# A hybrid diffusion step on one core: a planner with measured durations, load latencies and changes of matmul kind, and small products that are held back

## The chip, the cores and the metric

The kernel runs on one core of a Trainium2 chip. The metric is the device time of one execution in microseconds (us). Three executions of the kernel before took 1000.77, 1001.39 and 1002.3 us; the median is 1001.39 us.

## The reference, cut to what matters

A two-layer backbone is applied once to 128 context tokens and 256 latent tokens with shared weights (model width 1024). All 384 tokens are three tiles of 128 rows, t = 0 (context), 1 and 2 (latent).

```python
def trunk_layer(x, mod, p, lb_f, lb_b, rope, ctx_k, ctx_v, s0_f, s0_b):
    sh1, sc1, g1, sh2, sc2, g2 = jnp.split(mod, 6, axis=-1)      # mod = silu(c) @ w_mod + b_mod
    h = rmsnorm(x, p['norm1_g']) * (1 + sc1) + sh1
    proj = h @ p['w_in']                                          # 1024 -> 3328 columns
    q_r, f_f, f_b, i_r, g_r, q_a, k_a, v_a = jnp.split(proj, ...)
    ...
    o_f, s_f = gla_chunked(qr, -jnp.expm1(lf_f), vr, lf_f, s0_f)  # 4 recurrent heads, both directions
    o_b, s_b = gla_chunked(qr[:, ::-1], ...)
    ...
    o_a = attend_blocks(qa, k_all, v_all)                         # 8 query heads on 2 key heads
    x = x + g1 * (jnp.concatenate([o_r, o_a], axis=-1) @ p['w_out'])
    h2 = rmsnorm(x, p['norm2_g']) * (1 + sc2) + sh2
    x = x + g2 * (jnp.square(jax.nn.relu(h2 @ p['w1'])) @ p['w2'])   # 1024 -> 4096 -> 1024
```

The modulation `mod` needs 6144 columns of `w_mod` per layer for only two rows (`c_ctx` and `c`). The outputs are both normalised token sets, the keys and values of the context tokens, and their final recurrent states.

## The kernel before, in words

**Dense products.** A weight tile of 128 x 1024 numbers (512 KB) is loaded by SyncE into one of four `raw` buffers. ScalarE writes its high part as `hi` (L358), VectorE the rest as `lo` (L366), both in the type fp32r. Each product is then three fp32r matmuls: high by high, low by high, high by low. These are the lines L570 and L571 (queries and keys of the attention heads), L589 (the recurrent heads' features), L548 (their values and gates), L620 (w_out), L1124 and L1139 (w1) and L1150 (w2). They are called dense below.

**Small products.** The rest of TensorE's work is short groups in fp32: the modulation rows L413 (four products of `cT` with a raw `w_mod` tile, 256 columns each), L402 (the same rows where VectorE has summed them first at L382), the levels of the recurrence L936 and L922, its states and outputs L1011, L1034 to L1038, the attention scores L769 (fp32r on half of the array) and L807 and values L837, and transposes: L424, L494, L672, L731, L732, L791, L826, L1005, L1058, L1179. The trace shows two records for most of the fp32 products that the program holds, so eight at L413 are one weight tile's four.

**What sets the order.** Nothing on the chip decides: the program of each engine is a fixed list. It is written by a planner, `Sched`, when the kernel is built. Every piece of work is a step `S(engine, duration, function, r, w, acq, rel)`: keys that it reads and writes, buffers that it takes and gives back. Steps stand in chains (generators), and every chain has a priority. `start_of` (L51) works out when a chain's next step could start, from the free time of its engine, from the times of its keys plus a latency by engine (`LAT`), and from the free times of its buffers. `run` (L71) takes the earliest candidate, on VectorE, ScalarE and GpSimd with a window in which the priority counts (`BIAS`), calls its function, which emits the instructions, and books the time. A load is booked as busy for its duration on SyncE, and its data are taken to be there 1.6 us later: 1.47 us and 1.6 us for a 512 KB tile (L351).

**Around the change.** `load_chain` (L345) issues the weight tiles in one fixed order, each as soon as a `raw` buffer is free. A tile of `w_mod` gives its buffer back when L413 has read it; a tile of another weight when its `lo` is written. In layer 0 the tiles of three modulation blocks (eight each) stand between the tiles of `w_in`; the other blocks are summed by VectorE during the MLP of layer 0 (`mod_acc`, L382) and come to TensorE as L402. At the start a chain of matmuls on zeros (`warm_chain`, L272) keeps TensorE busy until the first dense product can run.

Of the kernel before, what the change touches and what calls it, by code (L numbers as in the profile page):

```python
# [14 lines left out]
NT = 3  # L15
# [5 lines left out]
LAG = HEAD + 1  # L21
WOT = 6
# [3 lines left out]
class Sched:  # L26


    LAT = {"PE": 0.2, "DVE": 0.19, "ACT": 0.13, "POOL": 0.15, "SP": 0.1}

    def __init__(self):
        self.free = {}
        self.t = {}
        self.slots = {}
        self.bound = {}
        self.chains = []
        self.n = 0

# [12 lines left out]
    def start_of(self, st):  # L51
        eng, dur, fn, r, w, acq, rel, key = st
        s = self.free.get(eng, 0.0)
        for k in r:
# [3 lines left out]
            s = max(s, te + (self.LAT[e] if e != eng else 0.0))  # L58
# [8 lines left out]
        return s  # L67

    BIAS = {"PE": (0.03, 0.0), "DVE": (0.96, 0.255), "ACT": (0.6, 0.255), "POOL": (0.8, 0.3), "SP": (0.03, 0.0)}

    def run(self):  # L71
        while self.chains:
            cand = []
            for c in self.chains:
                s = self.start_of(c[3])
                if s is not None:
                    cand.append((s, c))
            if not cand:
                raise RuntimeError("stuck: " + repr([(c[0], c[3][0], c[3][7], [k for k in c[3][3] if k not in self.t], c[3][5]) for c in self.chains]))
            pr = lambda c: c[0]() if callable(c[0]) else c[0]  # L80
            m, c = min(cand, key=lambda a: (a[0], pr(a[1]), a[1][1]))
            lim, w = self.BIAS[c[3][0]]
            s, c = min(((s, d) for s, d in cand if d[3][0] == c[3][0] and s <= m + lim), key=lambda a: ((a[0] - m if w else 0.0) + w * pr(a[1]), pr(a[1]), a[0], a[1][1]))
            eng, dur, fn, r, w, acq, rel, key = c[3]
# [6 lines left out]
            e = s + dur  # L91
            self.free[eng] = e
            lat = 0.0
            if eng == "SP":
                lat = 1.6
            for k in w:
                self.t[k] = (e + lat, eng)
            for name in rel:
                cls, o, i = self.bound.pop(name)
                self.slots[cls].append((e + lat, i, o))  # L100
# [7 lines left out]
def S(eng, dur, fn, r=(), w=(), acq=(), rel=(), key=None):  # L108
    return (eng, dur, fn, tuple(r), tuple(w), tuple(acq), tuple(rel), key)
# [10 lines left out]
def c_r(n):  # L120
    return max(n / 2400.0, 0.107)


def c_f(n, m=128):
    return max(n / 600.0, 0.214 * m / 128) + 0.004


def step_kernel(tc, A):
# [86 lines left out]
    def start_chain():  # L215
        yield S("SP", 0.9, lambda: SP.dma_start(out=cst, in_=A["cst"]), w=["smalls", "ident"])
# [20 lines left out]
        for t in range(NT):  # L237
            yield S("SP", 1.5, ldx(t), w=[("x", 0, t, 0), ("x", 0, t, 1)])

    def const_chain():  # L240
# [4 lines left out]
        yield S("SP", 2.0, ld2, r=[("rawk", 0, "feat", W_R0["q"])], acq=[("t2", "mraw")], w=["consts0"])  # L245
# [1163 lines left out]
```

## Time and profile before

| what | value |
|---|---|
| times of three executions, us | 1000.77, 1001.39, 1002.3 |
| profiled execution, us | 1002.09 |
| its span, from first to last instruction, us | 1000.3 |
| TensorE matmul busy, us (share) | 980.1 (98%) |
| VectorE busy, us (share) | 680.7 (68%) |
| ScalarE busy, us (share) | 495.6 (50%) |
| mean granted TensorE clock | 0.997 |
| moved by DMA | 165.40 MB, 165 GB/s over the span |

The span counts from the first to the last instruction; the profiled execution's own time is 1.8 us longer. PE is TensorE's matmul, PEld its weight loads, which overlap; DVE is VectorE, ACT ScalarE, POOL GpSimd, SP SyncE. A matmul's row gives its start, its length and what it reads and writes; since matmuls are pipelined, the distance between two starts tells what one costs, not its length. Where an engine sat idle before an instruction, the row ends with that time and with what released it.

### The profile page before, as it was taken

Reading aid. Unit: us, or ns where it says so; the run is one execution under the profiler, and the core shown is the slowest. Engines: PE = TensorE matmul, PEld = TensorE weight load, DVE = VectorE, ACT = ScalarE, POOL = GpSimd, SP = SyncE. Lnnn points to the kernel's source line nnn. Section 1 sums busy time; section 2 is a strip of 40 time slices with the busy share of each in tenths; the row PEclk is TensorE's granted clock in tenths of the full one; section 3 lists DMA queues with packets and bytes.
Section 4 is the critical chain, followed back from the end, with each engine's and each line's share of the span. In section 5 each row is a group of like instructions: output and inputs, shape, how many; then the busy total and the mean of one; then the engine's idle time right before and its main releaser. Section 6 shows DMA issues by size and latency. Waiting matters only on the chain.

```text
span 1000.3 us, 17353 instructions
## 1 busy us (share of the span) xinstructions
PE 980.1 (98%) x6925; PEld 836.4 (84%) x6925; DVE 680.7 (68%) x1169; ACT 495.6 (50%) x903; POOL 51.9 (5%) x49
## 2 busy tenths in 40 slices
PE   8999999999999999999999999999999999999997
PEld 5785677888989889888888978888899999999895
DVE  3687676687888889887746887977765444434434
ACT  4456644455544444444345677646564444444432
POOL 0020000111000000000011200011100000000002
PEclk9999999999999999999999999999999999999999
DMA  9958556333578767776615332242446544454611
GB/s 311 319 164 254 172 186 192 96 116 113 173 251 265 238 218 243 233 228 214 221 48 166 105 100 64 86 120 93 127 127 191 167 128 148 147 147 148 190 43 64
DMA packets 140657, 165.40 MB, mean 165 GB/s; under 512 B 5872, under 2 KB 105616, under 8 KB 140064
## 3 DMA queue, kind: packets, MB, share of 16 engines
q1 hardware_dynamic: 140576, 164.29, 53.0%
q8 instruction: 54, 0.88, 0.4%
q14 instruction: 27, 0.22, 0.1%
HBM read 161.35 MB, written 2.92 MB: 164 GB/s over the span
## 4 chain that ended last, share of the span: by engine, by line
PE 76%; DMA 11%; DVE 7%; issue 2%; ACT 2%; SPq 0%; POOL 0%; POOLq 0%; DVEq 0%; ACTq 0%
PE bank L1124 19%; PE bank L1150 19%; PE bank L589 9%; DMA raw<-w_mod_d 8%; PE bank L548 6%; PE bank L620 6%; DVE t L382 4%; PE bank L570 3%; PE bank L413 2%; PE bank L936 1%; PE bank L571 1%; DVE lo L366 1%; PE bank L1139 1%; PE bank L837 1%; DMA raw<-w_in_d 1%
## 5 line engine op out<-in xcount | busy, mean ns | idle before, releaser
L358 ACT CAST hi<-raw 128x1024 fp32r<-128x1024 f32 (+1 forms) x152 | 155.5, 1028 | 141.2 <-DMA raw<-w_d 69.4
L366 DVE TENSOR_TENSOR lo<-raw,hi 128x1024 fp32r<-128x1024 f32 (+1 forms) x152 | 179.6, 1192 | 44.9 <-ACT hi L358 44.5
L382 DVE SCALAR_TENSOR_TENSOR t<-raw,cT,t 128x512 f32<-128x512 f32 x196 | 135.4, 746 | 32.8 <-DMA raw<-w_mod_d 32.6
L1124 PE MATMUL bank<-mA,hi 128*128 128x384 f32 (+1 forms) x336 | 112.0, 333 | 0.0
L1124 PE MATMUL bank<-mA,lo 128*128 128x384 f32 (+1 forms) x336 | 111.1, 331 | 0.0
L1124 PE MATMUL bank<-mB,hi 128*128 128x384 f32 (+1 forms) x336 | 110.9, 330 | 0.0
L1112 DVE TENSOR_TENSOR mB<-t,mA 128x384 fp32r<-128x384 f32 x64 | 35.6, 556 | 96.0 <-ACT mA L1111 95.9
L1150 PE MATMUL bank<-lo,mA 128*128 128x512 f32 x252 | 98.8, 392 | 0.0
L1150 PE MATMUL bank<-hi,mB 128*128 128x512 f32 x252 | 98.7, 392 | 0.0
L1150 PE MATMUL bank<-hi,mA 128*128 128x512 f32 x252 | 98.0, 389 | 0.0
L1109 ACT ACTIVATE t<-bank 128x384 f32<-128x384 f32 x64 | 31.4, 490 | 125.3 <-PE bank L1124 122.8
L1124 PE MATMUL bank<-mA,wts 128*128 128x384 f32 (+1 forms) x352 | 88.7, 326 | 0.0
L1150 PE MATMUL bank<-wts,mA 128*128 128x512 f32 x264 | 87.7, 392 | 0.0
L358 ACT CAST wts<-raw 128x1024 fp32r<-128x1024 f32 x44 | 46.1, 1050 | 56.8 <-DMA raw<-w_d 21.3
L589 PE MATMUL bank<-Hh,hi 128*128 128x384 f32 x192 | 69.7, 363 | 0.6 <-ACT hg L866 0.6
L366 DVE TENSOR_TENSOR wts<-raw,wts 128x1024 fp32r<-128x1024 f32 x44 | 54.1, 1237 | 22.0 <-ACT wts L358 21.9
L1124 PEld LDWEIGHTS bank<-mA,hi 128*128 128x128 f32 x336 | 63.2, 188 | 3.1 <-issue 1.3
L589 PE MATMUL bank<-Hh,lo 128*128 128x384 f32 x192 | 64.8, 337 | 0.0
L589 PE MATMUL bank<-Hl,hi 128*128 128x384 f32 x192 | 64.6, 337 | 0.0
L1124 PEld LDWEIGHTS bank<-mB,hi 128*128 128x128 f32 x336 | 63.2, 188 | 1.4
L1124 PEld LDWEIGHTS bank<-mA,wts 128*128 128x128 f32 x352 | 62.5, 188 | 1.2 <-issue 0.4
L1124 PEld LDWEIGHTS bank<-mA,lo 128*128 128x128 f32 x336 | 63.2, 188 | 0.0
(252 smaller groups left out, 1955.5 us busy)
## 6 DMA issues: line engine op xcount, KB each, us to landing
raw<-w_d SPq DMA_DIRECT2D x128, 512.0 KB, 4.2
raw<-w_mod_d SPq DMA_DIRECT2D x80, 512.0 KB, 4.4
raw<-w_in_d SPq DMA_DIRECT2D x40, 512.0 KB, 4.6
raw<-w_in_d SPq DMA_DIRECT2D x16, 384.0 KB, 4.1
G<-grow SPq DMA_DIRECT2D x4, 1024.0 KB, 5.5
raw<-w_out_d SPq DMA_DIRECT2D x16, 256.0 KB, 4.3
raw<-w_out_d SPq DMA_DIRECT2D x8, 512.0 KB, 3.4
eB<-w_mod_d SPq DMA_DIRECT2D x12, 256.0 KB, 6.4
```

The costliest lines, as they stand in the source:

```text
L358: yield S("ACT", c_act(n), lambda u=u, n=n: ACT.copy(out=get(("hi",) + u)[:, 0:n], in_=get(("raw",) + u)[:, 0:n]), r=[("rawk",) + u] + ([( ...
L366: yield S("DVE", c_dve(n), lambda u=u, n=n: V.tensor_tensor(out=get(("lo",) + u)[:, 0:n], in0=get(("raw",) + u)[:, 0:n], in1=get(("hi",) + ...
L382: V.scalar_tensor_tensor(out=o, in0=raw, scalar=c, in1=o, op0=ALU.mult, op1=ALU.add)
L413: PE.matmul(get(nm)[32 * j:32 * j + m, 0:N], cT[:, k, 0:m], raw[:, o:o + N], start=k == 0, stop=k == 7, tile_position=(0, 32 * j))
L548: PE.matmul(ps, a, b, start=(first and k == 0 and i == 0), stop=(last and k == kk - 1 and i == 2))
L570: PE.matmul(get(aq), a, b[:, 0:512], start=st and i == 0, stop=sp and i == 2)
L589: PE.matmul(ps, a, b, start=(k == 0 and i == 0), stop=(k == 7 and i == 2))
L620: PE.matmul(ps, a, b, start=j == 0 and i == 0, stop=j == 7 and i == 2)
L1109: yield S("ACT", c_act(384, True), lambda: ACT.activation(out=get(r_)[:, 0:384], in_=get(z)[:, 0:384], func=AF.Relu), r=[z], acq=[("t2", r ...
L1112: yield S("DVE", c_dve(384), lambda: V.tensor_tensor(out=get(u)[1], in0=get(t_)[:, 0:384], in1=get(u)[0].bitcast(F32), op=ALU.subtract), r ...
L1124: PE.matmul(get(z)[:, cs], a, b, start=(k == 0 and i == 0), stop=(k == 7 and i == 2))
L1150: PE.matmul(get(("acc", l, "w2", t, hf)), a, b, start=(f == 0 and i == 0), stop=(f == NF - 1 and i == 2))
```

## The change

Only the planner and the numbers in the steps change; every step emits the instructions that it emitted before. The lines of the kernel after the change stand 26 lower in most places (L413 is L439, L589 is L615).

- Every step of TensorE has a kind: dense "d" (the default), "m" (fp32 products), "f" (small full ones), "t" (transposes), "w" (zeros at the start). A change of kind is booked with a time (`SWITCH`), between 0.01 and 0.2 us.
- Most small products have `hold=HOLD`, 1.0 us: while TensorE is in a dense run, they are sorted as if they could start 1.0 us later than they can. Once TensorE is in a small product, dense steps are sorted 0.15 us later (`STAY`), so that other small products that are due come first. The zeros at the start are sorted 0.3 us later.
- A load keeps SyncE for 0.1 us; its data pass one queue at 340 KB per us (`kb`), 1.3 us after the issue at the earliest, and count as there 1.8 us after that: 1.3 + 1.54 + 1.8 = 4.64 us for a 512 KB tile on an empty queue.
- TensorE's durations are new: a dense product of 384 columns is booked with 3 x 0.1733 us instead of 3 x 0.16 us, of 512 columns with 0.68 instead of 0.65 us; L413's four with 0.43 instead of 0.51 us.
- A step that reads what its own engine wrote waits a little (`OWN`).
- The first w_out steps wait for the end of all attention tiles (`att_done`) instead of their own tile's.

```diff
+HOLD = 1.0
+STAY = 0.15
...
+    OWN = {"PE": 0.0, "DVE": 0.06, "ACT": 0.14, "POOL": 0.1, "SP": 0.0}
+
+    SWITCH = {("d", "m"): 0.11, ("d", "f"): 0.1, ("d", "t"): 0.02, ("m", "d"): 0.2, ("f", "d"): 0.1, ("t", "d"): 0.09,
+              ("m", "t"): 0.09, ("m", "f"): 0.05, ("f", "m"): 0.09, ("f", "t"): 0.05, ("t", "m"): 0.09, ("t", "f"): 0.01}
+    DMA0, DMA1 = 1.3, 1.8
...
-            s = max(s, te + (self.LAT[e] if e != eng else 0.0))
+            s = max(s, te + (self.LAT[e] if e != eng else self.OWN[e]))
...
+        free = self.free.get(eng, 0.0)
+        if eng != "PE" or not dur:
+            s = max(s, free)
+            return s, s
+        if kind == "w":
+            return max(s, free), max(s, free) + 0.3
+        sw = self.SWITCH.get((self.kind, kind), 0.0)
+        v = max(s + hold, free) if self.kind == "d" else max(s, free) + (STAY if kind == "d" else 0.0)
+        return max(s, free) + sw, v
...
-            e = s + dur
-            self.free[eng] = e
-            lat = 0.0
-            if eng == "SP":
-                lat = 1.6
+            if eng == "SP" and dur:
+                self.free[eng] = s + 0.1
+                e = self.queue = max(s + self.DMA0, self.queue) + dur
+                e += self.DMA1
+            else:
+                e = self.free[eng] = s + dur
+            if eng == "PE" and dur:
+                self.kind = kind
...
+def kb(n):
+
+    return n * 1.024e-3 / 0.34
...
 def c_r(n):
-    return max(n / 2400.0, 0.107)
+    return max(n / 2400.0, 0.107) + 0.0133
...
-            yield S("SP", 1.12 if u[1] == "qk" else 1.47, f, r=...
+            yield S("SP", kb(384 if u[1] == "qk" else 512), f, r=...
...
-                yield S("PE", kk * (0.51 if N == 256 else 0.29), mm, r=...
+                yield S("PE", 0.43 if N == 256 else 0.5 if N == 128 and J == 4 else 0.55, mm, kind="m", hold=HOLD if N == 256 else 0.0, r=...
...
-            yield S("PE", 6 * (0.14 if m == 64 else 0.118), lambda: mm(m, nm), r=prev, acq=[("ps", nm)], w=[nm])
+            yield S("PE", 0.84 if m == 64 else 0.56, lambda: mm(m, nm), kind="m", hold=HOLD, r=prev, acq=[("ps", nm)], w=[nm])
...
-            mix = ("mixA", l, t) if j < 4 else ("mixR", l, g // 2, t)
-            return S("PE", 0.65, mm, r=...
+            mix = ("att_done", l) if j < 4 else ("mixR", l, g // 2, t)
+            return S("PE", 0.68, mm, r=...
```

What it does to the lists is seen at three places. The first is TensorE in layer 0, inside the last of the twelve feature tiles (L589), where the last modulation block before the MLP (its eight `raw` tiles, `cT` times each, the first of them with 32 rows) meets the recurrence (`hg`). Before:

```order
L413 MATMUL bank_62<-raw_116,cT 2x256 x4
L922 MATMUL bank_68<-hg_599 64x64 x12
L413 MATMUL bank_62<-raw_118,cT 2x256 x4
L589 MATMUL bank_67<-Hh,hi_122 128x384
L589 MATMUL bank_67<-Hl,hi_122 128x384
L589 MATMUL bank_67<-Hh,lo_126 128x384
...
L413 MATMUL bank_62<-raw_117,cT 2x256 x4
...
L1005 MATMUL bank_61<-cst,hg_599 128x128 x4
L413 MATMUL bank_62<-raw_116,cT 2x256 x4
L1005 MATMUL bank_64<-cst,hg_599 128x128 x4
```

And now, six dense matmuls later:

```order
L439 MATMUL bank_66<-raw_116,cT 32x256 x4
L948 MATMUL bank_63<-hg_603 64x64 x12
L439 MATMUL bank_66<-raw_117,cT 2x256 x4
L615 MATMUL bank_64<-Hh,hi_122 128x384
...
L439 MATMUL bank_66<-raw_115,cT 2x256 x4
L1031 MATMUL bank_61<-cst,hg_603 128x128 x4
L1031 MATMUL bank_62<-cst,hg_603 128x128 x4
L439 MATMUL bank_66<-raw_116,cT 2x256 x4
```

The block's first tile (`32x256`) now stands where its third stood; the third, the fifth and the sixth stood there before. The whole block comes later in the dense work, and its groups are gathered with neighbours.

The second place is TensorE a little further on, at the first values' tile (L548, now L574). Before, the block's last tile stood alone ahead of it:

```order
L589 MATMUL bank_67<-Hl,hi_122 128x384
L589 MATMUL bank_67<-Hh,lo_126 128x384
L413 MATMUL bank_62<-raw_117,cT 2x256 x4
L548 MATMUL bank_66<-hi_119,Hh 128x512
L548 MATMUL bank_66<-hi_119,Hl 128x512
L548 MATMUL bank_66<-lo_123,Hh 128x512
```

Now four groups stand together behind nine matmuls of that tile:

```order
L574 MATMUL bank_67<-lo_123,Hh 128x512
L439 MATMUL bank_66<-raw_118,cT 2x256 x4
L439 MATMUL bank_66<-raw_117,cT 2x256 x4
L962 MATMUL bank_63<-hg_545,ones 32x32 x24
L439 MATMUL bank_66<-raw_115,cT 2x256 x4
L574 MATMUL bank_67<-hi_119,Hh 128x512
```

The dense tile now starts ahead of the last four tiles of the block.

The third place is TensorE in the MLP of layer 0, where the fifth set of rows that VectorE has summed (`t`) is read. Before it stood inside the product with w1 (L1124, now L1150):

```order
L1124 MATMUL bank_65<-mA_2277,lo_123 128x384
L402 MATMUL bank_68<-t_6_113,sel 32x256 x2
L402 MATMUL bank_68<-t_1_108,sel 32x256 x2
L402 MATMUL bank_68<-t_3_110,sel 2x256 x2
L402 MATMUL bank_68<-t_7_114,sel 2x256 x2
L1124 MATMUL bank_65<-mA_2277,hi_119 128x384
```

Now it stands inside the product with w2 (L1150, now L1176) that follows:

```order
L1176 MATMUL bank_65<-lo_124,mA_2281 128x512
L428 MATMUL bank_68<-t_2_109,sel 32x256 x2
L428 MATMUL bank_68<-t_5_112,sel 32x256 x2
L428 MATMUL bank_68<-t_7_114,sel 2x256 x2
L428 MATMUL bank_68<-t_3_110,sel 2x256 x2
L1176 MATMUL bank_66<-hi_120,mA_2281 128x512
```

Counted over the program, 21 more dense matmuls stand ahead of this set than before (1776 instead of 1755). Over the whole list of TensorE, the dense work is interrupted by small products at 103 places instead of 118, of which those that hold "m" products alone are 43 instead of 51 and those of transposes alone 37 instead of 43. The zeros at the start are 30 matmuls instead of 20, and the first dense matmul stands behind 24 modulation matmuls instead of 32.

SyncE's list hardly changes: the order of the weight tiles is the same, and three constant loads and four stores stand one to three places elsewhere.

More of the change, by code (lines that the diff above doesn't have):

```diff
@@ L37, in __init__ @@
         self.n = 0
+        self.kind = "d"
+        self.queue = 0.0
     def add_slots(self, cls, objs):
@@ L66, in start_of @@
             s = max(s, sorted(f[0] for f in fs)[n - 1] + 0.15)
-        return s
-    BIAS = {"PE": (0.03, 0.0), "DVE": (0.96, 0.255), "ACT": (0.6, 0.255), "POOL": (0.8, 0.3), "SP": (0.03, 0.0)}
+        free = self.free.get(eng, 0.0)
[7 more added lines that the diff above has]
+        return max(s, free) + sw, v
     def run(self):
+        pr = lambda c: c[0]() if callable(c[0]) else c[0]
         while self.chains:
@@ L215, in start_chain @@
     def start_chain():
-        yield S("SP", 0.9, lambda: SP.dma_start(out=cst, in_=A["cst"]), w=["smalls", "ident"])
+        yield S("SP", kb(144), lambda: SP.dma_start(out=cst, in_=A["cst"]), w=["smalls", "ident"])
         def ini():
@@ L271, in warm_chain @@
         while until not in sch.t:
[L272 removed]
+            yield S("PE", 0.44 if n < cold else 0.22, kind="w", fn=lambda: PE.matmul(get(nm), z[:, 0:128], z[:, 0:512], start=True, stop=True), r=since, acq=[("ps", nm)] if n == 0 else [], w=[nm])
             n += 1
@@ L350, in f @@
                     SP.dma_start(out=view(raw), in_=src)
-            yield S("SP", 1.12 if u[1] == "qk" else 1.47, f, r=[("x", 0, t, 0) for t in range(NT)] + (["early"] if u in early else []), acq=[(rcls(u), ("raw",) + u)], w=[("rawk",) + u], key=u)
+            yield S("SP", kb(384 if u[1] == "qk" else 512), f, r=[("x", 0, t, 0) for t in range(NT)] + (["early"] if u in early else []), acq=[(rcls(u), ("raw",) + u)], w=[("rawk",) + u], key=u)
     def hi_chain():
@@ L1011, in mm @@
                 PE.matmul(get(p2)[:, i * 128:(i + 1) * 128], get(st)[:, i * 128:(i + 1) * 128], iSs[l][c][:, h * 128:(h + 1) * 128], start=True, stop=True)
-        yield S("PE", 4 * c_f(128), mm, r=[st] + [("iS", l, t) for t in range(NT)], acq=[("ps", p2)], rel=[st], w=[p2])
+        yield S("PE", 4 * c_f(128), mm, kind="f", hold=HOLD, r=[st] + [("iS", l, t) for t in range(NT)], acq=[("ps", p2)], rel=[st], w=[p2])
         def sm_():
@@ L1180, in mlp_head @@
         zs = [("z", l, 2 * p + j) for j in range(2)]
-        yield S("PE", 0.22, tr, r=[b] + [z + ("part",) for z in zs], rel=[b], w=zs)
+        yield S("PE", 0.22, tr, kind="t", r=[b] + [z + ("part",) for z in zs], rel=[b], w=zs)
     def final_chain(t):
```

81 lines of the change are left out of this document (40 added, 41 removed).

## The prediction

> **What bounds the kernel now.** The page comes first: the span, TensorE's busy share, the loads.
>
> ```profile
> span 1000.3 us, 17353 instructions
> PE 980.1 (98%) x6925; PEld 836.4 (84%) x6925; DVE 680.7 (68%) x1169; ACT 495.6 (50%) x903; POOL 51.9 (5%) x49
> raw<-w_mod_d SPq DMA_DIRECT2D x80, 512.0 KB, 4.4
> ```
>
> TensorE bounds the kernel, so a planner can win only where TensorE does nothing useful: in waits, and in what a change of work costs it. Second the table by stretches, to see where that can be (start and end of the stretch, its length, then each engine's busy time, and last the granted clock, the DMA share and GB/s).
>
> ```profile
> 75.00:100.00 25.00, 23.17 (x186) 14.44 (x182) 19.10 (x54) 17.43 (x53) 0.00 (x0) 1.00 0.81 254
> 100.00:125.00 25.00, 24.10 (x304) 16.92 (x301) 16.86 (x31) 15.72 (x28) 0.00 (x0) 1.00 0.55 172
> 125.00:150.00 25.00, 22.93 (x340) 19.56 (x339) 17.71 (x37) 12.16 (x18) 0.00 (x0) 0.95 0.57 186
> ```
>
> From 75 to 150 us, layer 0's attention and recurrence, 4.8 us of 75 are idle. Third, TensorE's waits (who, for whom: us in total, times, longest).
>
> ```profile
> PE bank L413 <- DMA raw<-w_mod_d: 4.6, 5, 2.0
> PE bank L402 <- DVE t L382: 1.4, 2, 0.9
> PE bank L570 <- DVE lo L366: 1.0, 2, 0.6
> PE bank L1011 <- ACT t L1007: 0.6, 2, 0.3
> PE bank L589 <- ACT hg L866: 0.6, 1, 0.6
> ```
>
> These 8.2 us are most of what TensorE waits between its first dense matmul and its last. More than half is a small product, L413, put in the list ahead of its tile's arrival, with dense work standing behind it that could have run.
>
> **Waits for loads.** The planner before took a 512 KB tile to be there 1.47 + 1.6 = 3.07 us after its issue; the page has 4.4 us as the median, so a group sorted to run at once stands 1.3 us early. The planner after takes 4.64 us and adds 1.0 us while dense work is there. A load with others beside it may take longer than 4.64 us, but the 1.0 us covers that for a group that opens a run of small products, not for one that joins a run. So of 4.6 us I take 3.7 as gone; the ends are 0 and 4.6.
>
> The longest of the five costs more than itself:
>
> ```profile
> 146.61 0.61 PE L413 MATMUL bank<-raw,cT 128*2 128x256 f32 x8 [1.97 <-DMA raw<-w_mod_d]
> ...
> 149.97 0.52 PE L589 MATMUL bank<-Hl,hi 128*128 128x384 f32 x1
> 150.29 0.52 PE L589 MATMUL bank<-Hh,lo 128*128 128x384 f32 x1
> ```
>
> The same place in the table by stretches:
>
> ```profile
> 146.00:149.00 3.00, 2.39 (x40) 1.47 (x40) 0.38 (x1) 0.29 (x1) 0.00 (x0) 0.72 0.50 142
> 149.00:152.00 3.00, 3.00 (x23) 1.83 (x16) 2.88 (x8) 1.90 (x6) 0.00 (x0) 0.71 0.71 246
> ```
>
> Behind it the granted clock is 0.72 and 0.71 for 5.4 us of work, and two dense matmuls that follow each other start 0.32 us apart. At full clock that work takes 0.28 x 5.4 = 1.5 us less. With the wait gone I take all 1.5 as gone; 0 if another wait of that length comes. The other four waits, of about 1 us or less, left the clock alone (1.00 from 75 to 125 us). The Trainium skill ("TensorE: Matmul & The Clock Gate", section "Why this matters for your kernels") asks only that TensorE not idle more than about 3 us between bursts; this trace loses clock after 1.97 us, so I go by the trace. By the rule this term would be 0.
>
> **Changes of kind.** A lone group of modulation products, a lone level of the recurrence, and the two together:
>
> ```profile
> 117.19 0.33 PE L589 MATMUL bank<-Hh,lo 128*128 128x384 f32 x1
> 117.46 0.61 PE L413 MATMUL bank<-raw,cT 128*2 128x256 f32 x8
> 118.00 0.45 PE L589 MATMUL bank<-Hh,hi 128*128 128x384 f32 x1
> 118.28 0.34 PE L589 MATMUL bank<-Hl,hi 128*128 128x384 f32 x1
> 118.46 0.33 PE L589 MATMUL bank<-Hh,lo 128*128 128x384 f32 x1
> ...
> 126.58 0.33 PE L589 MATMUL bank<-Hh,lo 128*128 128x384 f32 x1
> 126.85 0.63 PE L936 MATMUL bank<-hg 128*32 128x32 f32 x48
> 127.41 0.44 PE L589 MATMUL bank<-Hh,hi 128*128 128x384 f32 x1
> 127.69 0.34 PE L589 MATMUL bank<-Hl,hi 128*128 128x384 f32 x1
> ...
> 135.41 0.34 PE L589 MATMUL bank<-Hh,lo 128*128 128x384 f32 x1
> 135.68 0.64 PE L413 MATMUL bank<-raw,cT 128*32 128x256 f32 x8
> 136.14 0.64 PE L936 MATMUL bank<-hg 128*32 128x32 f32 x48
> 136.71 0.45 PE L589 MATMUL bank<-Hh,hi 128*128 128x384 f32 x1
> 136.99 0.34 PE L589 MATMUL bank<-Hl,hi 128*128 128x384 f32 x1
> ```
>
> Two dense matmuls without anything between start 0.175 us apart (118.28, 118.46). From the last dense start before to the second behind are 1.09, 1.11 and 1.58 us; less two such distances, the groups cost 0.74, 0.76 and 1.23 us. Together they are 0.27 us cheaper than apart. For transposes it is not so:
>
> ```profile
> 600.97 0.34 PE L589 MATMUL bank<-Hh,lo 128*128 128x384 f32 x1
> 601.14 0.81 PE L791 MATMUL bank<-cst,tok 128*128 128x128 f32 x6
> 601.97 0.34 PE L589 MATMUL bank<-Hl,hi 128*128 128x384 f32 x1
> ```
>
> That were six; here are twelve:
>
> ```profile
> 589.73 0.34 PE L589 MATMUL bank<-Hh,lo 128*128 128x384 f32 x1
> 589.90 1.58 PE L791 MATMUL bank<-cst,tok 128*128 128x128 f32 x12
> 591.49 0.33 PE L589 MATMUL bank<-Hl,hi 128*128 128x384 f32 x1
> ```
>
> Six cost 1.00 - 0.35 = 0.65 us, twelve 1.76 - 0.35 = 1.41, more than twice that. The list now has 103 interruptions instead of 118; those of "m" products alone fell by 8, those of transposes alone by 6. I take 8 x 0.27 = 2.2 us; the ends are 0 (all like transposes) and 15 x 0.27 = 4.1. The Trainium skill ("TensorE: Matmul & The Clock Gate", section "Step-by-step: what each phase is for") says that the drain of one matmul overlaps the fill of the next, so that back to back only the columns count. By that rule gathering pays nothing anywhere, and this term would be 0; the transposes agree with it, the two fp32 groups do not.
>
> **The other waits.** L402's rows stood in the list before VectorE had summed them. The fifth set now has 21 more dense matmuls ahead of it; at 0.175 us or more that is at least 3.7 us, four times the longest such wait. I take 1.4 of 1.4 us as gone; 0 is the other end, if VectorE's sums moved back as far. L1011 waits for ScalarE's copy of transposed states, and both are held back now; L866 is the first eviction of recurrent features, which frees a bank that the next tile needs; that tile now takes another bank. Of these 1.2 us I take 0.7; ends 0 and 1.2.
>
> **What it costs.** At the start the third token tile's transposes now stand ahead of all modulation products, and ScalarE squares that tile's second half behind two of the evictions of this row:
>
> ```profile
> 9.19 2.06 ACT L497 COPY xnT<-bank 128x512 f32<-128x512 f32 x4
> ```
>
> Two take 1.0 us, and the first dense matmul comes later by up to that. Eight modulation products also move behind it; by the rows above a group of four adds 1.23 - 0.76 = 0.47 us to a run, two groups 0.9. Together up to 1.9 us. But the loads set the pace there, and TensorE waits for a tile's split anyway (0.6 of L570's 1.0 us), so part is absorbed: I take 0.5; ends 0 and 1.9.
>
> A modulation tile read 1.0 us later gives its `raw` buffer back later. Behind it in SyncE's list stand the feature and value tiles of `w_in`, and dense matmuls wait for their split. With 24 tiles, 1.0 us each and four buffers, the stream of weights slips by at most 24 / 4 = 6 us, none of it on TensorE while tiles are ahead: the DMA share there is 0.55 to 0.81, and before no dense matmul waited for a split between 60 and 200 us. Also, every booked duration is now tight: before, a dense product was booked 8% short (0.48 us for what takes 3 x 0.175), which left the other engines that much time over; now only the 1.0 us is left. For both together I take 2.0 us of new waits; ends 0 and 6.
>
> **Sum**, against the profiled execution's 1002.09 us (span 1000.3 and 1.8 around it): -3.7 - 1.5 - 2.2 - 1.4 - 0.7 + 0.5 + 2.0 = -7.0 us. That execution is 0.7 us above the median of the three runs, so the median goes from 1001.39 to 994.4 us.
>
> **The rivals.**
>
> 1. The waits move instead of going. In a modulation block a buffer's cycle is issue, 4.4 us, product, next issue; if TensorE runs out of dense tiles while the block's last tiles are under way, it waits for the same loads later. For it: in the block at 144 us two groups are still put around L922 with nothing dense between. Against it: the loads at hand are the same, and dense work now stands first. Then only gathering, L402 and the start count: 1001.39 - 2.2 - 1.4 + 0.5 = 998.3 us.
> 2. Gathering pays nothing for the fp32 groups either, as it pays nothing in the transposes' rows: the time a dense matmul needs behind a small product would then be waiting of another kind. 994.4 + 2.2 = 996.6 us. The page's rule on drain and fill would have it so; the pair at 135.68 us speaks against it.
> 3. Slower: dense matmuls wait for their weights. Each of the three blocks is followed in SyncE's list by a tile that can be issued only when the block's buffers come back; it needs 4.4 us to land and then ScalarE and VectorE. In the second block the twelfth feature tile follows 48 dense matmuls behind the last product, 48 x 0.175 = 8.4 us. If it is late at all three blocks by 3 us, each such wait also costs the clock, 1.5 us: 3 x 4.5 = 13.5 us. The sum without its 2.0 us of new waits is -9.0, so the time is 1001.39 + 4.5 = 1005.9 us. It decides from three waits of 2 us on.
> 4. The change does not do what it says: 103 instead of 118 interruptions is little, and what is gained at the waits is given back at others of like size: 1001 us.
>
> **How the numbers follow.** The forecast has 0.53, rival 1 0.18, rival 2 0.10, rival 3 0.08, rival 4 0.11. About 0.2% (2 us) is what a measurement of this kernel can tell from no change. Forecast, rival 1 and rival 2 lie over 2 us below (0.81); less some of rival 1, which can end at nothing, faster is 0.78; same, with rival 4, 0.13; slower 0.09. The range: with all gains at their ends and no cost, 4.6 + 1.5 + 4.1 + 1.4 + 1.2 = 12.8 us, it is 988.6 us, which is unlikely as a whole, so it begins at 989.5; it reaches up over rivals 1 and 4 to 1001.5 us.
>
> **What would show it.** TensorE's waits: L413 for `w_mod` under 1 us in total, L402 gone; if they stand, the latencies were not the cause. The granted clock 1.00 from 125 to 175 us; if not, a wait of about 2 us is left. Busy TensorE less by some 2 us at equal instructions. L589 or L548 waiting for `lo` would be rival 3. It would be wrong at the root if the waits fell as said and the time did not.

## The result and the profile after

| | before | the change |
|---|---|---|
| median of four executions, us | 1001.85 | 994.37 |
| lowest to highest, us | 1000.77 to 1002.51 | 994.17 to 994.61 |
| profiled execution, us | 1002.09 | 994.49 |
| its span, us | 1000.3 | 992.7 |

The ratio is 0.9926, with a 95% interval from 0.9909 to 0.9944: 7.5 us faster. The forecast was 994.4 us. The sum was right; several of its terms were not. In the three series taken beside the experiments the kernel before had medians of 1002.87, 1001.64 and 1002.38 us, and single executions from 998.91 to 1008.39; each ratio below is to the series of its own run.

The page of the kernel after, span and busy engines:

```profile
span 992.7 us, 17368 instructions
PE 975.7 (98%) x6935; PEld 836.5 (84%) x6935; DVE 680.6 (69%) x1169; ACT 495.8 (50%) x903; POOL 49.5 (5%) x49
```

TensorE is busy 4.4 us less, with ten more matmuls (the zeros at the start). Not all of that is work: some 5 us before were waits that stand inside L402's groups as busy time, as shown below. The table by stretches, with its columns as before:

```profile
75.00:100.00 25.00, 24.89 (x197) 16.62 (x196) 18.89 (x53) 18.31 (x56) 0.00 (x0) 1.00 0.73 224
100.00:125.00 25.00, 25.00 (x350) 20.44 (x349) 20.69 (x39) 16.96 (x28) 0.00 (x0) 1.00 0.61 209
125.00:150.00 25.00, 25.00 (x329) 19.82 (x331) 18.14 (x37) 14.69 (x24) 0.00 (x0) 1.00 0.74 240
```

Of 75 us 0.1 are idle, where 4.8 were, and the granted clock is 1.00 throughout. TensorE's waits:

```profile
PE bank L520 <- DVE t L515: 2.4, 5, 1.2
PE bank L298 <- DVE sel L250: 2.1, 1, 2.1
PE bank L1084 <- DVE Hl L1089: 0.9, 1, 0.9
PE bank L596 <- ACT Hh L556: 0.8, 1, 0.8
PE bank L596 <- DVE lo L392: 0.7, 1, 0.7
PE bank L1084 <- DVE t L1079: 0.6, 2, 0.4
PE bank L948 <- ACT hg L977: 0.5, 1, 0.5
```

The rows for `w_mod` tiles (L413 before, L439 now) and for VectorE's sums (L402, now L428) are gone. L520, the transposes at the start, and L1084, the transposes that end the recurrence, are new in this size.

To see where the time comes from, the traces were laid side by side by their dense matmuls: both hold 4224, in the same order of work, so the start of the n-th in either trace marks the same point. Below, "before again" and "tail" are runs of the next section.

| n-th dense matmul starts at, us | before | before again | change | tail | change less before |
|---|---|---|---|---|---|
| first | 16.54 | 17.71 | 18.96 | 18.28 | +2.4 |
| 168 (early in layer 0) | 58.22 | 59.72 | 59.58 | 58.91 | +1.4 |
| 600 (in w_out, layer 0) | 215.10 | 215.02 | 210.19 | 206.55 | -4.9 |
| 2136 (early in layer 1) | 535.44 | 536.54 | 524.66 | 521.29 | -10.8 |
| 2800 (in w_out, layer 1) | 716.09 | 717.21 | 708.14 | 705.38 | -8.0 |
| 4200 (the end) | 987.49 | 988.61 | 979.88 | 977.13 | -7.6 |

Three pieces: 6.3 us gained in attention and recurrence of layer 0, 5.9 more up to the first products of layer 1, and 2.8 lost in layer 1. Against "before again" they are 4.7, 7.1 and 2.8: the first execution lost 1.5 us in layer 0 by a drop of the clock that the second had not (experiment 6), and the second lost 1.1 us more in the MLP. The prediction had looked for 1.4 us in the MLP.

There TensorE takes six sets of rows that VectorE has summed (L402). One of them before, from the list of instructions in order of time:

```profile
447.13 0.34 PE L1124 MATMUL bank<-mA,lo 128*128 128x384 f32 x1
448.38 2.50 PE L402 MATMUL bank<-t,sel 128*32 128x256 f32 x16 [0.91 <-DVE t L382]
450.80 0.44 PE L1124 MATMUL bank<-mA,hi 128*128 128x384 f32 x1
```

And one after:

```profile
444.33 0.40 PE L1176 MATMUL bank<-lo,mA 128*128 128x512 f32 x1
444.66 1.07 PE L428 MATMUL bank<-t,sel 128*32 128x256 f32 x16
445.66 0.50 PE L1176 MATMUL bank<-hi,mA 128*128 128x512 f32 x1
```

The sixteen records that take 1.07 us after took 2.50 before, and only the 0.91 us in front of them are listed as waiting. The rest lies inside the group: a matmul waits for its rows while the one ahead of it is still shown as running. From the start of the last dense matmul before to that of the first behind, the six sets took 14.4 us before and 7.7 after, 6.7 us less. The waits of the weight loads (PEld) show what TensorE's own rows hide. Before:

```profile
PEld bank L413 <- DMA raw<-w_mod_d: 8.8, 12, 2.3
PEld bank L402 <- DVE t L382: 5.1, 11, 0.6
PEld bank L402 <- ACT mA L1111: 1.3, 2, 0.9
```

That is 6.4 us for L402 where PE's list had 1.4, and 8.8 for L413 where it had 4.6. In the list after neither wait is among the first. Why VectorE was late is told by its own idle time, in the page's costliest groups. Before:

```profile
L382 DVE SCALAR_TENSOR_TENSOR t<-raw,cT,t 128x512 f32<-128x512 f32 x196 | 135.4, 746 | 32.8 <-DMA raw<-w_mod_d 32.6
```

After:

```profile
L408 DVE SCALAR_TENSOR_TENSOR t<-raw,cT,t 128x512 f32<-128x512 f32 x196 | 135.3, 746 | 7.6 <-DMA raw<-w_mod_d 7.6
```

The work is the same; before, VectorE stood idle 32.6 us ahead of it because its fixed list named a tile that had not landed.

### The profile page after: what moved, and what is told of

The parts are those of the page before. It is cut to its first block, busy times and chain, and to the rows that moved or that the text cites. A ratio compares the mean times of both kernels' runs of the same rounds, so it can differ in the third digit from the quotient of the medians.

```text
span 992.7 us, 17368 instructions
## 1 busy us (share of the span) xinstructions
PE 975.7 (98%) x6935; PEld 836.5 (84%) x6935; DVE 680.6 (69%) x1169; ACT 495.8 (50%) x903; POOL 49.5 (5%) x49
## 4 chain that ended last, share of the span: by engine, by line
PE 89%; DVE 3%; issue 2%; DMA 2%; ACT 2%; POOL 2%; SPq 0%; POOLq 0%; DVEq 0%; ACTq 0%
PE bank L1176 26%; PE bank L1150 25%; PE bank L615 10%; PE bank L574 6%; PE bank L646 4%; PE bank L596 3%; PE bank L439 2%; PE bank L597 2%; PE bank L962 1%; PE bank L863 1%; PE bank L1165 1%; PE bank L817 1%; PE bank L795 1%; DMA raw<-w_mod_d 1%; PE bank L520 1%
## 5 line engine op out<-in xcount | busy, mean ns | idle before, releaser
L1150 PE MATMUL bank<-mA,hi 128*128 128x384 f32 (+1 forms) x336 | 111.7, 332 | 0.0
L1150 PE MATMUL bank<-mA,lo 128*128 128x384 f32 (+1 forms) x336 | 111.1, 331 | 0.0
L1150 PE MATMUL bank<-mB,hi 128*128 128x384 f32 (+1 forms) x336 | 110.9, 330 | 0.0
L1176 PE MATMUL bank<-lo,mA 128*128 128x512 f32 x252 | 98.8, 392 | 0.0
L1176 PE MATMUL bank<-hi,mB 128*128 128x512 f32 x252 | 98.7, 392 | 0.0
L1176 PE MATMUL bank<-hi,mA 128*128 128x512 f32 x252 | 98.3, 390 | 0.0
L1150 PE MATMUL bank<-mA,wts 128*128 128x384 f32 (+1 forms) x352 | 89.7, 327 | 0.0
L1176 PE MATMUL bank<-wts,mA 128*128 128x512 f32 x264 | 86.8, 391 | 0.0
L615 PE MATMUL bank<-Hh,hi 128*128 128x384 f32 x192 | 68.0, 354 | 0.0
L1150 PEld LDWEIGHTS bank<-mA,hi 128*128 128x128 f32 x336 | 63.2, 188 | 2.2 <-issue 0.9
L615 PE MATMUL bank<-Hh,lo 128*128 128x384 f32 x192 | 64.5, 336 | 0.0
L615 PE MATMUL bank<-Hl,hi 128*128 128x384 f32 x192 | 64.4, 335 | 0.0
L1150 PEld LDWEIGHTS bank<-mB,hi 128*128 128x128 f32 x336 | 63.2, 188 | 1.4
L1150 PEld LDWEIGHTS bank<-mA,wts 128*128 128x128 f32 x352 | 62.6, 188 | 2.1 <-issue 1.3
L1150 PEld LDWEIGHTS bank<-mA,lo 128*128 128x128 f32 x336 | 63.2, 188 | 0.0
```

The costliest lines, as they stand in the source:

```text
L615: PE.matmul(ps, a, b, start=(k == 0 and i == 0), stop=(k == 7 and i == 2))
L1150: PE.matmul(get(z)[:, cs], a, b, start=(k == 0 and i == 0), stop=(k == 7 and i == 2))
L1176: PE.matmul(get(("acc", l, "w2", t, hf)), a, b, start=(f == 0 and i == 0), stop=(f == NF - 1 and i == 2))
```

## The experiments

All kernels but one are the changed kernel with parts undone or added; line numbers are its own, or three less where the load booking is undone, and 34 more in the MLP of the two probes (L1184 is w1, L1210 w2).

**1. The hold on the summed rows alone (e1).** The prediction had put L402's waits down to the dense matmuls that the hold lets pass.

```diff
-            yield S("PE", 0.9, mm, kind="m", hold=HOLD, r=[("modacck", ...
+            yield S("PE", 0.9, mm, kind="m", r=[("modacck", ...
```

> One part undone: the groups that read VectorE's sums (L428) are no longer held back; all else as changed. The traces say that these groups cost 14.4 us at six places of layer 0's MLP before and 7.7 us now, although the list of waits showed 1.4 us of waiting. Theory (the groups stood too early, and the wait is spread over their matmuls): the five or six groups move 3 to 30 dense matmuls forward, cost more again, 2 to 6 us of the 6.7 come back between dense matmuls 900 and 2000, about 998 us. Rival (the gain in the MLP comes from better load order or buffers, not from the hold): no change there, 994.4 us.

994.41 us (994.21 to 995.12), ratio to before 0.9914 (0.9883 to 0.9944): as the change. The six sets take 1.27 to 1.32 us each, as in the change (1.27 to 1.33). The rival holds: the hold on them does nothing for this gain. The fifth set even stands behind 1755 dense matmuls again, exactly where it stood before, and costs 1.27 us instead of 3.68.

**2. No hold and no changes of kind (e2).** Durations and load booking stay new.

```diff
-HOLD = 1.0
-STAY = 0.15
+HOLD = 0.0
+STAY = 0.0
...
-        sw = self.SWITCH.get((self.kind, kind), 0.0)
+        sw = 0.0
```

> No hold, no stay, no booked change of kind; measured durations and load latencies stay. The dense work is interrupted at 132 places instead of 103. Theory (gathering pays 0.27 us for each pair of fp32 groups, transposes nothing): of 29 more places 10 are m alone and 11 t alone, 6 f alone; 16 x 0.27 = 4.3 us, and the groups at VectorE's sums cost 2 to 6 us more: 1000 to 1004 us, waits for w_mod loads at L439 stay near 0.1 us since the latencies stay. Rival (the load latencies alone make the gain): within 1 us of 994.4.

998.90 us (997.26 to 1000.39), ratio 0.9958 (0.9941 to 0.9975). By these medians 4.5 us of the change need the gathering; 2.9 us are there without it (4.0 by the kernel before of the same series). The 1000 to 1004 us of the theory are missed, because the sums did not get dearer: the six sets take 1.27 to 1.33 us here too.

**3. The old load booking (e3).** A load again keeps SyncE for its whole transfer and is there 1.6 us later; the rest stays.

```diff
-            if eng == "SP" and dur:
-                self.free[eng] = s + 0.1
-                e = self.queue = max(s + self.DMA0, self.queue) + dur
-                e += self.DMA1
-            else:
-                e = self.free[eng] = s + dur
+            e = self.free[eng] = s + dur
+            if eng == "SP":
+                e += 1.6
```

> Only the booking of loads goes back to the old one (1.47 us on SyncE and 1.6 us to land); hold, kinds and durations stay. Theory of the prediction (the old latency put L413 1.3 us early, 3.7 us of waiting and 1.5 us of clock): waits at L439 for w_mod come back to 1 to 3 us since the hold of 1.0 us covers most of the 1.3 us; time 995 to 998 us. Rival (the hold alone is enough, and the new latencies cost at the start, where the first dense matmul comes 2.4 us later than before): no waits at L439, first dense matmul at about 16.5 to 17.5 us, 991 to 994 us.

1011.61 us (1007.29 to 1013.77), ratio 1.0079 (1.0050 to 1.0107): 17 us above the change, slower than before and outside both expectations. The six sets take 2.9 to 4.2 us each again, together 13.9 us more than in the change, and VectorE's idle time before its sums is back:

```profile
L405 DVE SCALAR_TENSOR_TENSOR t<-raw,cT,t 128x512 f32<-128x512 f32 x196 | 135.3, 747 | 46.5 <-DMA raw<-w_mod_d 46.1
```

The hold of 1.0 us does not cover a load that is booked 1.5 us short (1.54 + 1.6 = 3.14 us instead of 4.64).

**4. Prices of a lone group and of four together, and short waits (e4).** Probe groups are put between dense products of the second MLP block: groups of eight fp32 products as at L402 and groups of four transposes, four of each alone and four in a row, and transposes that wait for additions on GpSimd. Their results are not read, and the rest is computed as before.

```diff
+        def g_m(b):
+            for i in range(2):
+                for j in range(4):
+                    m = 32 if i == 0 else 2
+                    PE.matmul(b[32 * j:32 * j + m, 0:256], sel[...], rows[...], start=i == 0, stop=i == 1, tile_position=(0, 32 * j))
+        def g_t(b):
+            for j in range(4):
+                PE.transpose(b[:, j * 128:(j + 1) * 128], rows[...], ident)
...
+            yield from probe(f)
```

> The disputed prices by themselves, as extra work between dense products in the MLP of layer 1; it adds work whose results nothing reads. Four groups of eight small fp32 matmuls apart, then four such groups in a row; four groups of four transposes apart, then four in a row; then four waits of TensorE for GpSimd of growing length (256, 512, 768, 1024 columns, about 1.0, 1.7, 2.5 and 3.2 us). Theory: each fp32 group apart costs 0.27 us or more above its share in the row (0.8 us or more for four); the transposes nothing. The granted clock stays 1.00 behind the first and perhaps the second wait and falls to about 0.7 behind the third and fourth, for some 3 to 6 us, and costs 1 to 2 us each. Rival for gathering (the drain overlaps the fill): no difference in either. Rival for the clock: no fall after these waits; what fell at 146 us was the small fp32 work behind the wait, not the wait. About 994.4 + 8 x 0.9 + 8 x 0.45 + 9 + 2 x 1.5 = 1017 us.

1013.68 us, where about 1017 was expected. One group alone and four in a row, in order of time:

```profile
771.63 0.34 PE L1184 MATMUL bank<-mA,wts 128*128 128x384 f32 x1
771.90 1.07 PE L1146 MATMUL bank<-rows,sel 128*32 128x256 f32 x16
772.90 0.50 PE L1210 MATMUL bank<-wts,mA 128*128 128x512 f32 x1
773.24 0.40 PE L1210 MATMUL bank<-wts,mB 128*128 128x512 f32 x1
...
817.91 0.34 PE L1184 MATMUL bank<-mA,lo 128*128 128x384 f32 x1
818.18 3.66 PE L1146 MATMUL bank<-rows,sel 128*32 128x256 f32 x64
821.77 0.50 PE L1210 MATMUL bank<-hi,mA 128*128 128x512 f32 x1
822.11 0.40 PE L1210 MATMUL bank<-hi,mB 128*128 128x512 f32 x1
```

From the last dense start before to the second behind are 1.61 and 4.20 us; less the two dense distances, 0.40 us, a lone group costs 1.21 and four in a row 3.79. Apart they are 4.84, so each of the three joins saves 0.35 us. Four transposes, by the same reckoning, cost 0.44 us alone and 4 x 0.44 in a row: they save nothing. Behind waits of 0.75, 1.24, 1.94 and 2.36 us the granted clock stayed 1.00.

**5. Old durations (e5).** TensorE's steps are booked as before (three edits of nine are shown).

```diff
-    return max(n / 2400.0, 0.107) + 0.0133
+    return max(n / 2400.0, 0.107)
...
-                yield S("PE", 0.43 if N == 256 else 0.5 if N == 128 and J == 4 else 0.55, ...
+                yield S("PE", kk * (0.51 if N == 256 else 0.29), ...
...
-                    yield S("PE", 0.68, w2mm(f, t, hf), ...
+                    yield S("PE", 0.65, w2mm(f, t, hf), ...
```

> The changed kernel with one part undone: the planner's durations of TensorE steps are those of before (dense matmuls 8% shorter than the trace shows, some small groups longer). Load latencies, the hold and the changes of kind stay as in the change. Theory A (the load latencies carry the gain, the durations only matter together with them): with honest load latencies short durations make the planner believe that TensorE runs out sooner, so loads and VectorE's work are asked for in the same order or earlier; time within 3 us of the change, 992 to 998. Theory B (the two go together; one honest and one dishonest figure is worse than both old, as when the load latencies alone were put back and it took 1011.6): 1000 or more, with waits of dense matmuls for `lo` or of w_mod products for loads of over 3 us in all.

1017.40 us (1015.98 to 1020.00), ratio 1.0148 (1.0110 to 1.0185). Theory B. Up to the 2000th dense matmul it is 3.5 us behind the change, and 13.1 at the 2040th, near the end of the first MLP block; experiment 11 shows why. It loses 3.6 us more up to the 2136th and 5.1 from there to the 2800th, which no run looks into.

**6. The kernel before, once more (e6).** No edit.

> The kernel before once more, unchanged, to see which of its waits and which clock stretch are the program's and which are one execution's. Theory: the wait of L413 at 146 us stands again at 1.5 us or more, and the granted clock behind it is again under 0.8 for some 4 us. Rival: the wait stands, the clock is 1.00 behind it (as behind the wait of 1.96 us that the run with the old load figures had at 144.6 us), so the drop belongs to one execution and was never a loss that the change could take away. First dense matmul within 0.5 us of 16.5.

1003.21 us. The wait at 147 us is 1.15 us long, not 1.97, and the granted clock behind it is 1.00. So neither holds as written: the wait is shorter, and there is no drop behind it. The row of TensorE's waits:

```profile
PE bank L413 <- DMA raw<-w_mod_d: 3.8, 7, 1.2
```

TensorE in the table by stretches (busy time, clock, DMA share, GB/s):

```profile
146.00:148.00 2.00, 0.85 (x12) 1.00 1.03 386
148.00:150.00 2.00, 2.00 (x36) 1.00 0.58 134
```

The first dense matmul starts 1.2 us later than in the first execution, since the first token tile lands later: ScalarE's first square starts at 5.84 instead of 4.95 us (in the change's execution at 5.66). At the 600th dense matmul both are within 0.1 us, but that is a coincidence. The second execution is 0.9 to 1.8 us behind up to the 408th dense matmul. Its wait at 147 us is 0.8 us shorter, which leaves it 0.76 us behind; where the first then runs on its lower clock, it goes from 0.76 us behind to 0.72 ahead (151 us), and a wait at 155 us that the first has not takes back 0.6. So the drop cost the first execution 1.5 us, as the prediction had reckoned.

**7. The start's order (e7).**

```diff
-                    sch.spawn(g, 2 + 0.3 * t * 0.6 if l else 1 + 0.1 * t)
+                    sch.spawn(g, 2 + 0.3 * t * 0.6 if l else 0.3 if n_ == 0 else 1 + 0.1 * t)
```

> The changed kernel with one line more: the norm chains of layer 0 have priority 0.3 (first tile's chain stage), so the start's squares, transposes and w_mod products stand in the lists nearly in the order of before. Theory: the first dense matmul, 2.4 us later in the change than before, comes 1 us or more earlier than in the change, and at least 0.5 us of it reaches the end: 993.9 or less. Rival: loads set the pace of the first 50 us, the gain is gone by the 200th dense matmul, time 994.4 within 0.5, or other places that the planner then orders otherwise move it by up to 2 us either way.

995.07 us (993.79 to 995.54), ratio 0.9923 (0.9895 to 0.9950): nothing gained. In the profiled execution the second token tile landed late (ScalarE waits 1.37 us for it), so the trace can't tell what the order alone does; by the times it gives nothing back.

**8. and 9. The ends of the recurrence (e8, e9).** The hold is taken from two steps, the read-out's products (L1060) and the transposes behind them (L1084); e8 also has the line of experiment 7.

```diff
-        yield S("PE", (2 if t == 0 else 6) * c_f(128), mm, kind="f", hold=HOLD, r=r, ...
+        yield S("PE", (2 if t == 0 else 6) * c_f(128), mm, kind="f", r=r, ...
...
-        yield S("PE", 0.22, tr, kind="t", hold=HOLD, r=[y], ...
+        yield S("PE", 0.22, tr, kind="t", r=[y], ...
```

> As the run before, and in addition the hold is taken from two steps at the end of each recurrence (the fp32 products of the read-out and the transposes behind them, L1060 and L1084 in this count of lines). Theory: the change's waits at L1084 and L948 in front of the second dense block of each layer, together 2 to 3 us, go: between the last dense matmul of the features and 120 dense matmuls on it gains 1 us per layer, time 991 to 992.5. Rival: each step that is no longer held splits a run of small products, at 0.35 us for fp32 groups, and nothing is gained: 993.5 to 995.5.

> The changed kernel with the hold taken from two steps at the end of each recurrence alone (the fp32 products of the read-out, L1060, and the transposes behind them, L1084); nothing at the start is touched. Theory: the gain of the run before that had both edits (992.45 us, its gain in front of the 576th to 600th dense matmul) is this edit's, so 992 to 993 us, and the milestones lie within 0.5 us of that run from the 100th dense matmul on. Rival: it came from the start's line through the rest of the order, so 994 to 995.

e8: 992.45 us (992.00 to 993.71), ratio 0.9898 (0.9870 to 0.9926). e9: 992.41 us (991.74 to 993.12), ratio 0.9900 (0.9884 to 0.9917). So it is this edit, and the two are the fastest kernels here, 2.0 us below the change. What is gained lies at the end of layer 0's recurrence. The change, with the last transposes among the products of w_out:

```profile
206.01 0.82 PE L1084 MATMUL bank<-cst,t 128*128 128x128 f32 x6
207.69 0.44 PE L1084 MATMUL bank<-cst,t 128*128 128x128 f32 x2 [0.86 <-DVE Hl L1089]
208.01 0.50 PE L646 MATMUL bank<-hi,mAh 128*128 128x512 f32 x1
```

The same place in e9:

```profile
203.80 0.39 PE L646 MATMUL bank<-lo,mAh 128*128 128x512 f32 x1
204.03 0.60 PE L1084 MATMUL bank<-cst,t 128*128 128x128 f32 x4
204.38 0.48 PE L646 MATMUL bank<-hi,mAh 128*128 128x512 f32 x1
```

Held, the chain of read-out, square, scaling and transposes ends so late that its last two transposes need a bank that VectorE has just read (`Hl`), with TensorE waiting. In both kernels the last transposes stand behind the same number of dense matmuls, but in e9 four are left to do there instead of eight, and they don't wait. From the 552nd to the 600th dense matmul e9 gains 2.8 us on the change; three waits of the change there, of 0.32, 0.41 and 0.86 us, are not in e9's list, and the rest is not divided. In layer 1 the edit gains nothing (the 2.8 us lost there become 3.4).

**10. Hold and kinds alone (e10).** The edits of 3 and 5 together.

> Only the hold and the changes of kind: the planner's TensorE durations and the load booking are both those of before. Theory (durations and load figures must be wrong or right together, and the hold is worth some 4 us beside either pair): 996 to 999 us, with L402's groups (L425 in this count) still 2 us and more each in the first MLP block and VectorE idle for w_mod loads over 20 us in all. Rival (the gathering needs the right load figures, or else its held products wait for loads): 1001 or more.

1022.47 us (1020.26 to 1022.80), ratio 1.0196 (1.0175 to 1.0217). The rival: the slowest of all. Held products of modulation wait for their loads again:

```profile
PE bank L436 <- DMA raw<-w_mod_d: 7.3, 7, 1.9
```

Ahead of one of them TensorE stands still for 3.77 us, for which the row names no releaser:

```profile
103.42 1.08 PE L436 MATMUL bank<-raw,cT 128*32 128x256 f32 x8 [3.77 <-issue]
...
106.17 0.52 PE L612 MATMUL bank<-Hl,hi 128*128 128x384 f32 x1
106.49 0.52 PE L612 MATMUL bank<-Hh,lo 128*128 128x384 f32 x1
```

Behind it two dense matmuls start 0.32 us apart instead of 0.17: the clock is halved.

**11. The load booking alone (e11).** The edits of 2 and 5 together.

> Only the new load booking: the TensorE durations are those of before, no hold, no changes of kind. With durations and loads both new and no hold it took 998.9; with hold and loads but old durations 1017.4. Theory (the mismatch of durations and loads is what costs, hold or not): 1010 to 1022, dense matmuls waiting for `hi` and `lo` of w_down tiles at the end of the first MLP block for 4 us or more. Rival (the mismatch costs only together with the hold, since held steps are timed against the wrong clock): 997 to 1003.

1010.30 us (1007.77 to 1012.14), ratio 1.0074 (1.0047 to 1.0102). The theory: the mismatch costs without the hold too. Three of TensorE's longest waits in it, at the end of the first MLP block and just behind it:

```profile
PE bank L596 <- DVE lo L392: 2.9, 2, 2.3
PE bank L1176 <- ACT wts L384: 2.6, 1, 2.6
PE bank L1176 <- ACT hi L384: 1.6, 1, 1.6
```

VectorE's sums between 440 and 510 us tell why (count, then shortest, median and longest ns, then first and last start). In the change:

```profile
L408 DVE SCALAR_TENSOR_TENSOR t<-raw,cT,t x32: 742/747/753, 440.3 to 480.3; 128x512 f32<-128x512 f32 x32
```

In e11:

```profile
L408 DVE SCALAR_TENSOR_TENSOR t<-raw,cT,t x48: 739/746/748, 439.9 to 503.2; 128x512 f32<-128x512 f32 x48
```

Ahead of the 2030th dense matmul, near the end of the block, the last of these sums starts 17.5 us earlier in the change, 2.3 in e11 and 2.8 in e5. Until a tile of `w_mod` is summed it holds one of the four `raw` buffers, so the block's last four tiles of `w_d` are issued from 494 us on, where in the change the last was by 481, and the dense matmuls wait for their split.

**12. Longer waits (e12).** Only the GpSimd probes of experiment 4, with longer additions; their results are not read.

```diff
+            for m in [512] * (n // 512) + [n % 512] * (n % 512 > 0):
+                PO.tensor_tensor(out=scr[:, 0:m], in0=scr[:, 0:m], in1=scr[:, 0:m], op=ALU.add)
```

> The changed kernel with four extra waits of TensorE inside the dense matmuls of the second MLP block (a transpose that waits for GpSimd's additions; results unread), about 2.4, 3.0, 3.6 and 4.7 us long. Behind the waits of 0.75 to 2.36 us of an earlier run the granted clock stayed at 1.00. Theory (length decides, with a bound above 2.4 us): the clock behind one or more of the longer ones falls under 0.8 for some 4 us, and it stays 1.00 behind the first. Rival (only a thin stretch of small products does it, as at 146 us in the kernel before): 1.00 behind all four. Time: 8 groups of small work and 13.7 us of waits, 1009 to 1014.

1016.78 us (1009 to 1014 was expected); the waits were 2.29, 3.24, 3.67 and 5.65 us. Behind each of the four the clock falls, behind the first like this:

```profile
882.76 0.33 PE L1156 MATMUL bank<-cst,scr 128*128 128x128 f32 x1 [2.29 <-POOL scr L1155]
...
883.87 0.63 PE L1210 MATMUL bank<-hi,mB 128*128 128x512 f32 x1
884.30 0.63 PE L1210 MATMUL bank<-lo,mA 128*128 128x512 f32 x1
...
886.86 0.57 PE L1210 MATMUL bank<-lo,mA 128*128 128x512 f32 x1
887.26 0.39 PE L1210 MATMUL bank<-hi,mA 128*128 128x512 f32 x1
```

Eight distances take 3.39 us instead of 8 x 0.227 = 1.82: half the clock for 3.4 us, 1.6 us lost. Yet the wait of 2.36 us of experiment 4, at the same kind of place, cost none, while shorter ones elsewhere brought a drop: 1.74 us in e10, 1.88 in e5, and in e2 two of 0.63 and 1.27 us that end 2.1 us apart. Length alone does not decide up to 2.4 us, and neither theory holds as written.

**The parts together.** Each row is one kernel; ranges and ratios stand above.

| hold and kinds | TensorE durations | load booking | median, us | kernel |
|---|---|---|---|---|
| no | old | old | 1001.85 | before |
| no | old | new | 1010.30 | e11 |
| no | new | new | 998.90 | e2 |
| yes | old | old | 1022.47 | e10 |
| yes | old | new | 1017.40 | e5 |
| yes | new | old | 1011.61 | e3 |
| yes | new | new | 994.37 | the change |

Old durations cost 23.0 us beside hold and new loads and 11.4 without the hold; the old load booking costs 17.2 beside hold and new durations. Holding back costs 20.6 us with both old figures and gains 4.5 with both new ones. (The rows but the first keep the change's small edits, such as `OWN` and `att_done`. New durations with old loads and no hold was not run.)

## Why the prediction was right or wrong

**Waits for loads, -3.7: right, a little small.** L439 waits 0.1 us for loads where L413 waited 4.6. That the latencies were the cause is shown by e3, where 4.3 us of such waits are back (six times, 2.0 at the longest). What stood in the weight loads' list was 8.8 us; no run tells how much of the rest reached the end.

**The clock, -1.5: right for the two profiled executions, not for the kernel.** The sign came, 1.00 from 125 to 175 us. In the first execution the drop cost 1.5 us, by the comparison with e6. But e6 also shows that not every execution has the drop, and in e3 a wait as long as the first left the clock alone:

```profile
144.62 0.61 PE L436 MATMUL bank<-raw,cT 128*2 128x256 f32 x8 [1.96 <-DMA raw<-w_mod_d]
```

The stretch behind it:

```profile
145.00:147.00 2.00, 2.00 (x63) 1.00 0.64 207
```

The prediction took all of it off the median; how many of the other executions had a drop is not on record. The Trainium skill ("TensorE: Matmul & The Clock Gate", section "What's actually happening") describes a free-running activity window of about 3.4 us that sets the clock, so that what happens depends on where in it the work lands. The runs agree with that: 3.4 us of half clock in e12, and waits of 1.7 to 2.4 us with either outcome. Its rule that it takes an idle window of that length does not fit, since 2.29 us were enough.

**Changes of kind, -2.2: right mechanism, price low.** A join saves 0.35 us (e4) where 0.27 was read from one pair, transposes nothing, as read. Eight joins are 2.8 us, by an estimate. Against e2, which has ten places of "m" products alone more than the change, ten joins would be 3.5 of the 4.5 us. The rest no run divides: e2 also waits for `t` and `Hh` at L615 and L596, 2.7 us together, and its profiled execution has a drop of the clock at 64 us.

**The other waits, -1.4 for L402: wrong size, wrong cause.** "The fifth set now has 21 more dense matmuls ahead of it" was the argument. e1 and e2 have no hold on these rows, the fifth set at its old place, and the same gain; e3 has the hold and not the gain. It is the load booking, through VectorE's list, and it is 6.7 us, not 1.4: the list of TensorE's waits showed a fifth of it. The row on VectorE's 32.6 idle us stood in the page and was passed over as idle time off the bottleneck. The waits at L1011 and L866 are both gone (1.2 us, where 0.7 was taken), and L948 and L596 wait 0.5 and 0.8 instead.

**The start, +0.5: too small, and its absorption is not shown.** The first dense matmul is 2.4 us later, of which 0.7 is the token tile's landing in this execution (5.66 against 4.95 us). Less the difference in landing, the order's part is 1.4 us against e6 and 1.7 against the first execution, by an estimate: within the ends (0 and 1.9), and more than the 0.5. At the 168th dense matmul the change is level with e6 (0.1 us ahead), but it is 0.6 us behind at the 156th and again at the 204th, since small groups stand at other places. And "before again" is still 1.6 us behind the first execution at 143 us, where its shorter wait for a load takes up 0.8. So it is not shown that the loads absorbed the change's late start. e7 did not bring it back.

**New waits, +2.0: another cause, and less than was lost.** No dense matmul waits for `lo` between 60 and 200 us. What the change loses is held work at the end of layer 0's recurrence, 2.0 us by e9, and 2.8 us in layer 1. The second was in no term, and its cause stays open: e2, which holds nothing back, is 1.5 us longer than before in the same stretch, so the hold can be the cause of a part only. And "every booked duration is now tight" was counted as a cost; e5 and e11 show that without the tight durations the new load booking does not pay at all.

**The rivals.** Rival 1: the waits did not come back elsewhere in the block. Rival 2 falls with the 0.35 us. Rival 3 is not here, but its mechanism is what e5 and e11 lose by: dense matmuls wait for split weights, up to 2.6 us each, and the clock falls behind some. Rival 4 named waits of like size; there are some at the start and at the recurrence's end, and they give back part only.

**The sum.** That it came out near the result is luck in part. L402 gave 5.3 us more than was put down, and a loss of 2.8 us in layer 1, which no term held, took back half of that. The terms as measured (-4.5 loads, -1.5 clock, -2.8 joins, -6.7 sums, +1.4 at the start, +4.8 lost) add up to -9.3 us where the two profiled executions are 7.6 apart; they overlap, or something is lost where no run looks.

## What to carry to other kernels

A planner's figures belong together: one right figure beside a wrong one cost 8 to 16 us against the kernel before, in which both were wrong, and a rule such as holding work back paid only where both were right. It looks as if two errors had cancelled; new durations alone, without the hold, were not run. Where an in-order engine off the critical path stands idle for loads ahead of something the bottleneck reads, that idle time is worth following. Read the waits of the weight loads beside TensorE's own, and compare a group's time from dense start to dense start, since waits inside a run of small matmuls do not show as idle time.

## What the hardware showed that was not expected

- A wait of TensorE of about 2 us may or may not halve its clock: 1.74, 1.88, 1.97 and 2.29 us did, 1.87, 1.96 and 2.36 us did not; 3.24 us and more did. The clock is halved for 3.41 us each time, or for twice that (6.83 us behind the wait of 5.65, of which about half fell into the wait itself); the drop behind 2.29 us cost 1.6 us.
- Two executions of one program differ by 0.9 us in when the first token tile lands and by 1.2 us in the first dense matmul. They are level at the 600th only because one had a drop of the clock, and 1.1 us apart again at the 2136th.
- A group of eight fp32 products costs 1.21 us alone among dense matmuls and 0.95 in a row; transposes cost 0.11 us each either way.
